# Seven products instead of eight for three retention output units, with sums kept in DRAM, in a one-core hybrid trunk layer

## The chip, the cores and the metric

The kernel runs on one core of one Trainium2 chip. The metric is the device time of one execution in microseconds (us), as the median of several runs. One execution is also recorded by the hardware profiler; all rows of a profile come from that one.

The engines are named as in the profile: PE is TensorE (PEld its weight loads), DVE is VectorE, ACT is ScalarE, POOL is GpSimd, SP is SyncE, whose queue issues nearly all DMA transfers.

## The reference: what is computed

One layer on a sequence of 1024 positions and width 1024, all in float32. Cut to what matters:

```python
h = rms_norm(x, norm1_w)
q, k, v, g_ret, x_lru, y_lru, gate_ret, gate_lru = split(h @ w_in)
o = chunkwise_retention(rotary(q), rotary(k), v)             # 4 heads
y_a = (head_group_norm(o) * silu(g_ret)) @ w_ret_o           # retention output
hl = rg_lru(causal_depthwise_conv(x_lru))                    # recurrent block
y_b = (hl * gelu(y_lru)) @ w_lru_o                           # recurrent output
mix = sigmoid(gate_ret + b0) * y_a + sigmoid(gate_lru + b1) * y_b
x = x + mix @ w_out
h = rms_norm(x, norm2_w)
gate, val = split(h @ ffn_w_up)
x = x + (gelu(conv(gate)) * val) @ ffn_w_down
return rms_norm(x, norm_f_w)
```

The change concerns the product with w_ret_o and the order in which the columns of w_in are worked off.

## The kernel before, in words

**Units and products.** Every large product is cut into units of 256 output channels by all 1024 positions, with 1024 terms to a sum. Activations lie with channels on the partitions, so a unit's operand has four blocks: B11, B12, B21, B22 (first index: half of the terms; second: half of the positions), each of four tiles of 128 x 512. The unit's weights are four blocks A11 to A22 of 128 x 512. Each float32 tile is split into a rounded high part and a rest (`split`: a cast on ACT, a subtraction on DVE), and a product of two tiles is three matmuls (`PASSES`).

A unit runs in one of two forms. `mm_std` computes the four results directly. `mm_fast` uses seven products of blocks in place of eight: the weights give sums S1 to S4, made for each unit on DVE (`preps`, L271 to L287), and the operand gives sums T1 to T4, made once for each operand, when at least one of its units is fast. In the fast form a bank is copied out three times on ACT (`keep`, L432) and three results are summed on DVE (`total`, L443). `FAST_RO` and `FAST_LO` say how many of the four units of the retention output and of the recurrent output are fast: 0 and 3 before.

**Stages.** The input stage has 28 units: eight gate units g, four y and four x units (y_lru and x_lru), and three units for each head h0 to h3. Their order is the string `SEQ`. All are fast but the first two. Then follow the retention output's four units (called o0 to o3 here), the recurrent output's four (l0 to l3), the output projection and the feed-forward part. Between stages the operand changes: the normed input h1 first, then og (the gated retention output, written to the DRAM buffer og_d by `ret_out`), then u (written to u_d by `lru_block`). The results of the gate units go through a sigmoid (`emit_gate`, L1015) to sg_d, those of the y units through a gelu (`emit_y`, L810) to y_d.

**Background work.** The work of the heads and of the recurrent blocks (`rotary_head`, `retention_head`, `ret_out`, `lru_block`) is written as generators, which wait in one line (`back`). After each product of a fast unit, and eight times in a standard unit, `advance(RATE)` lets the first of them go on until its steps have used up a budget of 1 times the number of generators in line. A recurrent block enters the line when its x unit is done; a head's three parts after its three units. `u_start`, which runs after o2, empties the line and then queues the building of u.

A second line, `builders`, makes the operands for the next stage: `operand` reads the 16 tiles of an operand back from DRAM, up to eight tiles ahead, and splits them. It starts for og when the last but one input unit is done (`og_start`). `build` stops while fewer than 20 buffers are free (`RESERVE`); a product that lacks a tile makes it at once (`need`). The instructions of builders, bank copies and totals get a higher priority than their place in the program.

**Buffers and queues.** All tiles of 128 x 512 outside the weights come from one pool of 81 buffers (`U`), used in the order in which they were given back. A full operand with its sums takes 32 + 32 of them. At the last unit on an operand each block is given back after the product that used it; B12 goes before the first fast unit. Each engine works through its instructions in order, and so does SP's queue: a store waiting for its data holds up the loads behind it. Weights (pool `W`) are loaded six tiles ahead.

**Kept sums.** In the feed-forward part the operand of the down projection is a weight. Its sums T1 to T4 are made early by `down_sums`, kept in the DRAM buffer td_d and read back and split by `down_op`. In the profile, x_d and t_d are the buffers x1_d and t1_d of the code.

Of the kernel before, what the change touches and what calls it, by code (L numbers as in the profile page):

```python
# [11 lines left out]
F32 = mybir.dt.float32  # L12
# [5 lines left out]
P = 128  # L18
D = 1024
T = 1024  # L20
KT = 8
TH = 512
# [64 lines left out]
class Units:  # L87
# [11 lines left out]
    def get(self, dt=F32):  # L99
        i = self.q.popleft()  # L100
        self.count += 1
        t = self.pool.tile(self.shape, dt, tag=f"{self.name}{i}", name=f"{self.name}{i}_{self.count}")
        self.at[id(t)] = (i, t)
        return t

    def put(self, *tiles):
        for t in tiles:
            self.q.append(self.at.pop(id(t))[0])
# [28 lines left out]
RESERVE = 20  # L137
LAG, AHEAD_B, AHEAD_T = 2, 7, 4
NOW, SOON, OLD = 3000, 400, 800
FAST_RO = 0  # L140
RO_T = 9
FAST_LO = 3
GQ = False
SEQ = "g g y0 g y1 h0 h1 h2 h3 x0 g g x1 g y2 g x2 g y3 x3"
STD_L = 2


# [1 line left out]
def tile_trunk_layer(ctx, tc, x, xt, positions, params, consts, normf, w_in, w_ro, w_lo,  # L149
                     w_out, w_up, w_dn, w_gate, out):  # L150
    nc = tc.nc
    V, S, G, PE, SY = nc.vector, nc.scalar, nc.gpsimd, nc.tensor, nc.sync
    ST = G if GQ else SY
# [3 lines left out]
    pdr = ctx.enter_context(tc.tile_pool(name="dr", bufs=1, space=bass.MemoryType.DRAM))  # L157
# [6 lines left out]
    get, put = U.get, U.put  # L164
# [3 lines left out]
    ident = cst[:, C_ID:C_ID + P]  # L168

    og_d = pdr.tile([KT, P, T], F32, tag="og", name="og_d")  # L170
    u_d = pdr.tile([KT, P, T], F32, tag="u", name="u_d")
    y_d = pdr.tile([KT, P, T], F32, tag="y", name="y_d")
    sg_d = pdr.tile([2, KT, P, T], F32, tag="sg", name="sg_d")
# [2 lines left out]
    td_d = pdr.tile([3, 4, 4, P, TH], F32, tag="td", name="td_d")  # L176
# [8 lines left out]
    def split(src, get=get, S=S, V=V):  # L185

        hi, lo = get(F32R), get(F32R)
        S.copy(hi, src)  # L188
        V.tensor_sub(lo, src, hi.bitcast(F32))  # L189
        return hi, lo  # L190
# [3 lines left out]
    BS, BV = Behind(tc, S), Behind(tc, V)  # L194
# [112 lines left out]
    builders = deque()  # L307
# [34 lines left out]
    def drain():  # L342
        while back:
            advance(1e9)
# [156 lines left out]
    def pair_src(w, i):  # L501
        return lambda m, kh: w[i, 2 * m + kh]
# [58 lines left out]
    def reads(fetch, keys, ahead):  # L561

        keys, got = deque(keys), deque()
        while keys or got:
            while keys and len(got) <= ahead:
                got.append((state["tick"], fetch(*keys.popleft())))
            yield got.popleft()

    def landed(tick):

        while state["tick"] - tick < LAG and not state["force"]:
            yield 0

    def tsets(op, fetch, ahead=AHEAD_T, here=False):
        tiles = reads(fetch, [(n, j) for j in range(4) for n in ("B11", "B12", "B21", "B22")], ahead)
        for j in range(4):
            four = [next(tiles) for _ in range(4)]
            if not here:
                yield from landed(four[-1][0])
            b11, b12, b21, b22 = (t for _, t in four)  # L580
            t1, t2 = get(), get()
            BV.tensor_sub(t1, b12, b11)
            op["T1", j] = split(t1, get, BS, BV)
            yield 1.2
            BV.tensor_sub(t2, b22, t1)
            op["T2", j] = split(t2, get, BS, BV)
            yield 1.2
            BV.tensor_sub(b12, b12, b22)
            op["T3", j] = split(b12, get, BS, BV)
            BV.tensor_sub(t2, b21, t2)  # L590
            op["T4", j] = split(t2, get, BS, BV)
            put(t1, t2, b11, b12, b21, b22)
            yield 2.4
# [11 lines left out]
    h1, keep = {}, {}  # L605
# [292 lines left out]
    qk, vv, gg = {}, {}, {}  # L898
# [31 lines left out]
    def retention_head(hd, qk, vv):  # L930
        cur = 0
        mask = cst[:, C_MASK + 128 * hd:C_MASK + 128 * hd + 128]
        for h in range(2):
# [55 lines left out]
                yield 0.3  # L989
            put(kd[h], vt[h, 0], vt[h, 1], qk[0, h], qk[1, h])  # L990

    def ret_out(hd, gg):
        for h in range(2):
            for m in range(2):
                ps = psa.get()
                for b in range(4):
                    c0 = 256 * (b % 2) + 128 * m
                    PE.transpose(ps[:, 128 * b:128 * b + 128], ob[h, b // 2][:, c0:c0 + 128], ident)
                g = gg[m, h]
                V.scalar_tensor_tensor(g, ps, pc("ret_gn_w", 2 * hd + m), g, ALU.mult, ALU.mult)  # L1000
                psa.put(ps)
                ST.dma_start(og_d[2 * hd + m, :, TH * h:TH * h + TH], g)
                put(g)
                yield 0.8
            put(ob[h, 0], ob[h, 1])
        if hd == HEADS - 1:
            put(*rot.values())
# [13 lines left out]
    def operand(op, fetch, sums=True):  # L1021

        keys = [(n, j) for n in ("B11", "B21", "B12", "B22") for j in range(4)]
        for key, (tick, t) in zip(keys, reads(fetch, keys, AHEAD_B)):
            yield from landed(tick)
            op[key] = split(t, get, BS, BV)
            put(t)
            yield 0.6
        if sums:
            yield from tsets(op, fetch)  # L1030

    def from_dram(src):
        def fetch(n, j):
            t = get()
            h = int(n[2]) - 1
            SY.dma_start(t, src[4 * (int(n[1]) - 1) + j, :, TH * h:TH * h + TH])
            return t
        return fetch

    og, u = {}, {}  # L1040
# [16 lines left out]
    def emit_ret_o(n):  # L1057
        def emit(m, h, ps, unit):
            ch = 2 * n + m
            t = ojobs[n].take(m, h)  # L1060
            V.tensor_mul(t, ps, t)
            ST.dma_start(t1_d[ch, :, TH * h:TH * h + TH], t)
            put(t)
            if unit is not None:
                put(unit)
        return emit
# [33 lines left out]
    for what in SEQ.split():  # L1100
        if what == "g":
            add_gate()
        elif what[0] == "y":
            n = int(what[1])
# [10 lines left out]
    jobs[-1].last = True  # L1115
    def og_start(post=jobs[-2].post):
        builders.append(operand(og, from_dram(og_d), False))
        return post() if post else None

    jobs[-2].post = og_start  # L1120

    def og_sums():
        drain()
        if FAST_RO:
            builders.append(tsets(og, from_dram(og_d)))

    def u_start():
        drain()
# [1 line left out]

    ojobs = []
    for n in range(4):
        ojobs.append(Job(pair_src(w_ro, n), og, emit_ret_o(n), {2: u_start, RO_T: og_sums}.get(n),
                        fast=n >= 4 - FAST_RO, last=n == 3, drop12=n == 3 - FAST_RO, fetch=from_sg(0, n)))
    for n in range(4):
        ojobs.append(Job(pair_src(w_lo, n), u, emit_lru_o(n), fast=n >= 4 - FAST_LO, last=n == 3,
# [128 lines left out]
    def down_op(g):  # L1265
        def fetch(n, j):
            t = get()
            kh, c = int(n[1]) - 1, int(n[2]) - 1
            SY.dma_start(t, w_dn[8 * g + 4 * kh + j, :, TH * c:TH * c + TH])
            return t  # L1270

        yield from operand(dop[g], fetch, False)

        def sums(n, j):
            t = get()
            SY.dma_start(t, td_d[g, int(n[1]) - 1, j])
            return t

        keys = [(f"T{i}", j) for i in (1, 2, 3, 4) for j in range(4)]
        for key, (tick, t) in zip(keys, reads(sums, keys, AHEAD_B)):  # L1280
            yield from landed(tick)
            dop[g][key] = split(t, get, BS, BV)
            put(t)
            yield 0.6

    def down_sums(g, j):

# [169 lines left out]
```

## Time and profile before

| | us |
|---|---|
| median of 3 runs (1656.72 to 1660.0) | 1659.52 |
| profiled execution, its own time | 1658.44 |
| profiled execution, span from first to last instruction | 1656.7 |

The span is shorter than the execution's own time because it has only what lies between the first and the last instruction. The mean granted clock of PE was 0.997 of full speed.

Where the stages lie in the profiled execution, from PE's timeline:

| stage | from us | to us |
|---|---|---|
| input stage, 28 units | 0 | 657 |
| o0 to o3 and l0 (PE L360, standard form) | 657 | 781 |
| l1 to l3 (PE L417, fast form) | 781 | 844 |
| output projection (PE L1221, its last result added by DVE L1223) | 844 | 938 |

In rows of the profile an instruction carries the line of the kernel that made it, or the line of a helper: L188 and L189 are the two halves of `split`, L122 the same when called for an operand by a builder, L852 the gate matmuls of a recurrent block, L360 and L417 the matmuls of the standard and the fast form. A releaser ("<-ACT u L432") is the instruction that ended the idle time before. Idle time of an engine that is not the bottleneck costs nothing.

### The profile page before, as it was taken

The numbers are of one execution on the slowest core, as the hardware profiler recorded it, in microseconds if no ns is written. First come the engines' busy times: TensorE is split into PE (matmuls) and PEld (weight loads), VectorE is DVE, ScalarE is ACT, GpSimd is POOL, SyncE is SP. The second block draws the span as 40 slices with busy tenths as digits, with TensorE's granted clock in tenths as the row PEclk, the third lists the DMA queues.
The fourth block names the chain that finished last, engine by engine and source line by source line (L and its number), as shares of the span: only waits on it lengthen the run. The fifth ranks groups of instructions, "written<-read, shape, count | busy, mean of one in ns | idle before, by whom it ended". The sixth has DMA issues, their size and how long they took to land. (4 is left out here: it accounts for less than half of the span.)

```text
span 1656.7 us, 21338 instructions
## 1 busy us (share of the span) xinstructions
PE 1622.3 (98%) x7224; PEld 1329.8 (80%) x7224; DVE 1287.0 (78%) x2366; ACT 880.2 (53%) x1480; POOL 40.6 (2%) x60
## 2 busy tenths in 40 slices
PE   8999999999999998999999999999999999999997
PEld 6788888888888877888778778888888887888886
DVE  8998767676888888958871798777777767877786
ACT  7664444535677866853440464444444545453554
POOL 0001000000000000000000000000000000000000
PEclk9999999999999999999999999999999999999999
DMA  8243223131332337658462144444444456778761
GB/s 296 81 161 102 73 68 90 45 96 45 104 119 95 134 122 251 213 171 268 153 215 89 65 150 163 138 134 135 139 143 139 156 160 218 260 262 264 267 203 77
DMA packets 134350, 251.16 MB, mean 152 GB/s; under 512 B 15584, under 2 KB 15712, under 8 KB 134240
## 3 DMA queue, kind: packets, MB, share of 16 engines
q1 hardware_dynamic: 130016, 236.16, 43.9%
q0 software_dynamic: 4224, 13.64, 2.2%
q8 instruction: 56, 0.92, 0.2%
q14 instruction: 54, 0.44, 0.1%
HBM read 177.38 MB, written 67.11 MB: 148 GB/s over the span
## 5 line engine op out<-in xcount | busy, mean ns | idle before, releaser
L417 PE MATMUL g<-u,w 128*128 128x512 f32 x5124 | 1204.0, 393 | 14.9 <-ACT u L432 13.3
L417 PEld LDWEIGHTS g<-u,w 128*128 128x128 f32 x5124 | 958.2, 188 | 218.7 <-ACT u L432 18.6
L188 ACT CAST w<-w 128x512 fp32r<-128x512 f32 x471 | 291.3, 620 | 413.2 <-PE g L417 286.9
L189 DVE TENSOR_TENSOR w<-w,w 128x512 fp32r<-128x512 f32 x471 | 321.9, 684 | 83.4 <-ACT w L188 73.7
L360 PE MATMUL g<-u,w 128*128 128x512 f32 x960 | 223.5, 390 | 0.0
L360 PEld LDWEIGHTS g<-u,w 128*128 128x128 f32 x960 | 179.3, 188 | 38.0 <-ACT u L686 0.3
L443 DVE TENSOR_TENSOR u<-g,u 128x512 f32<-128x512 f32 x183 | 125.3, 685 | 50.5 <-PE g L417 40.4
L432 ACT COPY u<-g 128x512 f32<-128x512 f32 x183 | 106.1, 580 | 65.0 <-PE g L417 62.8
L122 DVE TENSOR_TENSOR u<-u,u 128x512 fp32r<-128x512 f32 (+1 forms) x192 | 122.0, 683 | 15.1 <-ACT u L122 10.4
L122 ACT CAST u<-u 128x512 fp32r<-128x512 f32 x160 | 90.4, 619 | 45.0 <-DVE u L122 15.3
L1221 PE MATMUL g<-u,u 128*128 128x512 f32 x384 | 90.0, 392 | 1.0 <-ACT u L188 0.9
L1221 PEld LDWEIGHTS g<-u,u 128*128 128x128 f32 x384 | 71.3, 188 | 16.6 <-ACT u L188 1.4
L1254 DVE SCALAR_TENSOR_TENSOR u<-u,par,u 128x511 f32<-128x511 f32 x96 | 71.6, 745 | 4.1 <-ACT u L1251 3.4
L1259 POOL DMA_DIRECT2D ff_d<-u x48 | 36.1, 752 | 1251.7 <-DVE u L1258 1251.7
L271 DVE TENSOR_TENSOR w<-w,w 128x512 f32<-128x512 f32 x61 | 42.0, 689 | 25.3 <-DMA w<-ff_d 9.6
L188 ACT CAST u<-u 128x512 fp32r<-128x512 f32 x72 | 43.3, 619 | 26.5 <-DMA u<-w_out 11.2
L1251 ACT ACTIVATE u<-u,par 128x512 f32<-128x512 f32 x48 | 39.2, 817 | 28.2 <-DVE u L443 27.5
L852 PE MATMUL a<-u,u 128*128 128x512 f32 x192 | 48.7, 393 | 2.5 <-ACT u L188 1.6
L189 DVE TENSOR_TENSOR u<-u,u 128x512 fp32r<-128x512 f32 x72 | 47.9, 683 | 4.0 <-ACT u L188 3.7
L1223 DVE TENSOR_TENSOR u<-g,u 128x512 f32<-128x512 f32 x16 | 10.9, 690 | 48.2 <-PE g L1221 48.2
L852 PEld LDWEIGHTS a<-u,u 128*128 128x128 f32 x192 | 35.5, 188 | 12.0 <-ACT u L188 3.1
L274 DVE TENSOR_TENSOR w<-w,w 128x512 f32<-128x512 f32 x61 | 41.9, 687 | 1.0
(175 smaller groups left out, 1211.7 us busy)
## 6 DMA issues: line engine op xcount, KB each, us to landing
w<-w_in SPq DMA_DIRECT2D x112, 256.0 KB, 2.7
w<-w_up SPq DMA_DIRECT2D x96, 256.0 KB, 2.7
u<-w_dn SPq DMA_DIRECT2D x96, 256.0 KB, 3.2
u<-x_d SPq DMA_DIRECT2D x56, 256.0 KB, 5.0
x_d<-u SPq DMA_DIRECT2D x48, 256.0 KB, 3.5
ff_d<-u POOLq DMA_DIRECT2D x48, 256.0 KB, 2.9
td_d<-u SPq DMA_DIRECT2D x48, 256.0 KB, 3.3
w<-ff_d SPq DMA_DIRECT2D x48, 256.0 KB, 4.3
```

Source lines behind the costliest of these rows:

```text
L122: ins = fn(*args, **kw)
L188: S.copy(hi, src)
L189: V.tensor_sub(lo, src, hi.bitcast(F32))
L271: V.tensor_add(s1, a21, a22)
L274: V.tensor_sub(s1, s1, a11)
L360: PE.matmul(ps[h], w[a][:, c], o[b], start=n == 0, stop=n == 23)
L417: PE.matmul(bank, w[a][:, c], need(op, (bn, j))[b], start=first and n == 0, stop=n == 11, skip_group_check=True)
L432: BS.last = S.copy(u, bank).ins.name
L443: BV.last = V.tensor_add(u, bank, u).ins.name
L852: PE.matmul(ps, wg[g][a][:, cs], xs[k][b], start=q == 0, stop=q == 5)
L1221: PE.matmul(ps, o[a][:, 128 * t:128 * t + 128], wo[k][b], start=n == 0, stop=n == 23)
L1254: V.scalar_tensor_tensor(c[:, s:], src[:, :TH - s], w, c[:, s:], ALU.mult, ALU.add)
```

## The change

Three of the four retention output units become fast (`FAST_RO = 3`); o0 stays standard. The sums T1 to T4 of og are not made when og is read back, but in the background line while heads 2 and 3 are finished: `out_sums` reads the tile of head 0 or 1 back from og_d, subtracts it with the two tiles of head 2 or 3, which are still in buffers, and stores four sums to the new DRAM buffer to_d. `kept_sums`, taken out of `down_op` with the same instructions as before, reads them back and splits them after og's own tiles. The order `SEQ` changes: y1 follows y0 at once, x0 to x3 stand three units apart each, and x3 is followed by two gate units that end the stage.

```diff
-FAST_RO = 0
-RO_T = 9
+FAST_RO = 3
...
-SEQ = "g g y0 g y1 h0 h1 h2 h3 x0 g g x1 g y2 g x2 g y3 x3"
+SEQ = "g g y0 y1 h0 h1 h2 h3 x0 y2 g x1 y3 g x2 g g x3 g g"
...
+    to_d = pdr.tile([4, 4, P, TH], F32, tag="to", name="to_d")
...
+    def out_sums(j, b21, b22):
+
+        b11, b12 = get(), get()
+        for h, b in ((0, b11), (1, b12)):
+            SY.dma_start(b, og_d[j, :, TH * h:TH * h + TH])
+        yield 1.0
+        V.tensor_sub(b11, b12, b11)
+        ST.dma_start(to_d[0, j], b11)
+        yield 0.6
+        V.tensor_sub(b12, b12, b22)
+        ST.dma_start(to_d[2, j], b12)
+        put(b12)
+        yield 0.6
+        V.tensor_sub(b11, b22, b11)
+        ST.dma_start(to_d[1, j], b11)
+        put(b22)
+        yield 0.6
+        V.tensor_sub(b21, b21, b11)
+        ST.dma_start(to_d[3, j], b21)
+        put(b21, b11)
+        yield 0.6
+
     def ret_out(hd, gg):
...
                 ST.dma_start(og_d[2 * hd + m, :, TH * h:TH * h + TH], g)
-                put(g)
                 yield 0.8
+                if hd < 2:
+                    put(g)
+                elif h == 1:
+                    yield from out_sums(2 * hd - 4 + m, gg[m, 0], g)
...
+    def kept_sums(op, src):
+
+        def fetch(n, j):
+            t = get()
+            SY.dma_start(t, src[int(n[1]) - 1, j])
+            return t
+
+        keys = [(f"T{i}", j) for i in (1, 2, 3, 4) for j in range(4)]
+        for key, (tick, t) in zip(keys, reads(fetch, keys, AHEAD_B)):
+            yield from landed(tick)
+            op[key] = split(t, get, BS, BV)
+            put(t)
+            yield 0.6
...
         builders.append(operand(og, from_dram(og_d), False))
+        builders.append(kept_sums(og, to_d))
         return post() if post else None
...
-        ojobs.append(Job(pair_src(w_ro, n), og, emit_ret_o(n), {2: u_start, RO_T: og_sums}.get(n),
+        ojobs.append(Job(pair_src(w_ro, n), og, emit_ret_o(n), {2: u_start}.get(n),
                         fast=n >= 4 - FAST_RO, last=n == 3, drop12=n == 3 - FAST_RO, fetch=from_sg(0, n)))
...
+        yield from kept_sums(dop[g], td_d[g])
```

More of the change, by code (lines that the diff above doesn't have):

```diff
@@ L1117, in og_start @@
         builders.append(operand(og, from_dram(og_d), False))
+        builders.append(kept_sums(og, to_d))
         return post() if post else None
     jobs[-2].post = og_start
[L1122 to L1125, printed above, removed]
     def u_start():
@@ L1272, in down_op @@
         yield from operand(dop[g], fetch, False)
[L1274 to L1284, printed above, removed]
+        yield from kept_sums(dop[g], td_d[g])
     def down_sums(g, j):
```

## The prediction

> **What bounds the kernel now.** I read the busy totals first, then the busy time by stretch, then the timeline of TensorE inside the stretches that the diff touches, and last the timelines of ScalarE and SyncE at its longest stop. (The chain of waits is no help here: the pieces it lists start at 1391 us, long after the code that changes.)
>
> ```profile
> span 1656.7 us, 21338 instructions
> ...
> PE 1622.3 (98%) x7224; PEld 1329.8 (80%) x7224; DVE 1287.0 (78%) x2366; ACT 880.2 (53%) x1480; POOL 40.6 (2%) x60
> ```
>
> TensorE (PE) is busy 1622.3 of 1656.7 us; only 34.4 us of the span are not matmuls. VectorE (DVE) is second with 78%. An average can hide a stage with another limit, so here is the run in stretches. The columns are: window, its length, then busy us and (instructions) of PE, weight load, DVE, ACT and POOL, the granted TensorE clock, the DMA share and GB/s.
>
> ```profile
> 20.00:140.00 120.00, 120.00 (x526) 98.18 (x525) 118.57 (x257) 75.31 (x133) 4.29 (x8) 1.00 0.47 156
> 140.00:440.00 300.00, 298.49 (x1424) 246.31 (x1423) 217.90 (x471) 138.55 (x247) 0.00 (x0) 1.00 0.24 70
> 440.00:643.00 203.00, 200.50 (x880) 164.36 (x879) 176.01 (x300) 157.46 (x228) 0.00 (x0) 1.00 0.40 131
> 643.00:657.00 14.00, 9.25 (x34) 7.18 (x33) 8.81 (x15) 8.70 (x17) 0.00 (x0) 0.88 0.87 291
> 657.00:844.00 187.00, 182.51 (x799) 149.08 (x798) 153.41 (x252) 107.51 (x160) 0.00 (x0) 1.00 0.62 202
> ```
>
> They are the start, the four heads, the recurrent blocks, the seam from the input stage to the retention output (o0 to o3), and the two output projections (o0 to o3, then l0 to l3). In every one of them PE is the busiest engine, except at the seam. Two things matter for what follows. DVE at 99% (20 to 140 us) did not cost PE anything: PE was busy 120.00 of 120. And the output stretch already uses 153.41 of 187 us of DVE.
>
> The rows of PE's timeline give the price of a matmul and of the seam (start, length, what, idle time before it):
>
> ```profile
> 571.20 32.80 PE L417 MATMUL g<-u,w 128*128 128x512 f32 x144
> 603.84 0.39 PE L852 MATMUL a<-u,u 128*128 128x512 f32 x1
> ...
> 649.29 4.61 PE L417 MATMUL g<-u,w 128*128 128x512 f32 x12 [4.75 <-ACT u L432]
> ...
> 656.92 6.05 PE L360 MATMUL g<-u,w 128*128 128x512 f32 x26
> ```
>
> From 571.20 to 603.84 run 144 matmuls without a gap: 32.64/144 = 0.2267 us each (the 390 ns of a single record overlap the next one). At the seam PE stands for 4.75 us, and the next twelve take 4.61 us where 12 x 0.2267 = 2.72 are due: 1.9 more. The seam costs 4.75 + 1.9 = 6.6 us. Why it stands, from SyncE and ScalarE:
>
> ```profile
> 635.59 3.95 SPq L1036 DMA_DIRECT2D u<-og_d  x2
> ...
> 642.43 0.50 SPq L811 DMA_DIRECT2D y_d<-u  x1
> ```
> ```profile
> 648.13 0.62 ACT L122 CAST u<-u 128x512 fp32r<-128x512 f32 x1 [3.32 <-DMA y_d<-u]
> 648.66 0.58 ACT L432 COPY u<-g 128x512 f32<-128x512 f32 x1
> ```
>
> The copy that frees PE's bank (L432) stands in ScalarE's queue behind a split of the new operand (L122). That split wants a buffer which a store to y_d still holds, and the store was issued at 642.43, behind reads of og_d. So it is a shortage of buffers at a change of operand, passed on by in-order queues.
>
> **The change, part by part.** *Removed from PE.* A four-bank unit is 2 x 2 x 8 x 3 = 96 matmuls, a seven-product unit 7 x 12 = 84. Three units change: 36 x 0.2267 = **-8.2 us**. This work is on PE, which sets the time in that stretch, so it counts in full unless PE then waits.
>
> *Added to DVE and ACT in the output stage.* Prices:
>
> ```profile
> L188 ACT CAST w<-w 128x512 fp32r<-128x512 f32 x471 | 291.3, 620 | 413.2 <-PE g L417 286.9
> L189 DVE TENSOR_TENSOR w<-w,w 128x512 fp32r<-128x512 f32 x471 | 321.9, 684 | 83.4 <-ACT w L188 73.7
> ...
> L443 DVE TENSOR_TENSOR u<-g,u 128x512 f32<-128x512 f32 x183 | 125.3, 685 | 50.5 <-PE g L417 40.4
> L432 ACT COPY u<-g 128x512 f32<-128x512 f32 x183 | 106.1, 580 | 65.0 <-PE g L417 62.8
> ...
> L271 DVE TENSOR_TENSOR w<-w,w 128x512 f32<-128x512 f32 x61 | 42.0, 689 | 25.3 <-DMA w<-ff_d 9.6
> ```
> ```profile
> 650.59 2.49 DVE L122 TENSOR_TENSOR u<-u,u 128x512 fp32r<-128x512 f32 x4
> ```
>
> Per fast unit: three more splits of weights, four sums of weights (L271 and the like), three bank sums (L443), three bank copies (L432). With 16 splits of the kept sums that is 16 + 3 x 10 = 46 DVE operations. One lasts 0.684 us, but four back to back take 2.49, so the next starts after (2.49 - 0.68)/3 = 0.60: 27.7 to 31.5 us of DVE. ACT gets 25 casts and 9 copies, 25 x 0.62 + 9 x 0.58 = 20.7 us, on top of 107.51 in 187: it does not bind.
>
> *Moved: two gate units behind x3.* Each product spends one unit of budget per waiting background generator, and the steps of one lru_block add up to 35.2. Followed through the old order, o0 starts with 43.0 steps outstanding (7.8 of block 2 and all of block 3); in the new order with 23.8. So 19.2/35.2 = 55% of a block leaves the stretch. The old count is borne out by the blocks' gate matmuls inside it, 66 of the 48 per block, 1.4 blocks against 43.0/35.2 = 1.2:
>
> ```profile
> 657.00:844.00 187.00, 16.21 (x66) 12.31 (x66) 1.00 0.62 202
> ```
>
> What a block costs DVE, from the groups of 440 to 643 us:
>
> ```profile
> L835 DVE SCALAR_TENSOR_TENSOR u<-u,par,u 128x511 f32<-128x511 f32 (+2 forms) x30 | 22.2, 743 | 0.0
> ...
> L864 DVE TENSOR_TENSOR u<-u,u 128x512 f32<-128x512 f32 x10 | 6.9, 689 | 7.7 <-ACT u L855 7.7
> ...
> L885 DVE TENSOR_TENSOR_SCAN u<-u,st,u 128x512 f32<-128x512 f32 x4 | 5.1, 1279 | 0.0
> L872 DVE TENSOR_SCALAR u<-u 128x512 f32<-128x512 f32 x10 | 4.2, 422 | 0.1
> ```
>
> Four tiles, each with three L835, five operations like L864, one L872, one scan and one split: 4 x (2.2 + 3.4 + 0.4 + 1.3 + 0.7) + 2 splits = 33 us, of which 55% are 18. DVE in the stretch becomes 153.4 + 27.7 (31.5) - 18 = 163 to 167 us. PE there becomes 187 - 8.2 - 0.55 x 48 x 0.2267 = 173 us. DVE at 94 to 97% of PE's time: tight, but the row of 20 to 140 us shows PE unhurt at 99%. Without the moved gates DVE would need 181 to 185 against 179 and bind. The PE work of the gates and of the block is only shifted: 0.
>
> *Added in the input stage.* Four out_sums, each two reads of og_d, four subtractions and four stores: 16 subtractions at the price of the like ones for the down weights,
>
> ```profile
> L1299 DVE TENSOR_TENSOR u<-u,u 128x512 f32<-128x512 f32 x12 | 8.3, 689 | 8.6 <-DMA u<-w_dn 8.6
> ```
>
> are 11 us beside 82 us of idle DVE in the heads' stretch (300 - 217.9). SyncE gets 24 issues there and 16 reads of to_d later, at most 0.50 us each by the store above (12 and 8 us), and its stores wait for subtractions with weight loads queued behind them; six weight tiles are loaded ahead, more than a unit's worth (19 us). Hidden: 0, and if that cover fails one stall as at the seam, 6.6. Starting the heads one unit earlier runs them closer to the rotary tables, on a DVE at 99%: 0 by the same row.
>
> *The seams.* (a) Input stage to o0: same mechanism as before, with the sigmoid store of a gate in place of y_d's. Its cost stays; from -6.6 (two gates store and free buffers early) to +6.6 (block 3 is in work at the same time and holds more). I take 0. (b) The kept sums are needed one product after o1 begins. Nearest rows: the same seam at l0 to l1, where sums are made on the spot, and the change of group in the down stage, where they are kept:
>
> ```profile
> 786.71 0.96 PE L417 MATMUL g<-u,w 128*128 128x512 f32 x3 [0.95 <-ACT u L432]
> 788.27 2.60 PE L417 MATMUL g<-u,w 128*128 128x512 f32 x10 [0.59 <-ACT u L122]
> 791.78 44.67 PE L417 MATMUL g<-u,w 128*128 128x512 f32 x194 [0.92 <-DVE u L122]
> 838.47 5.78 PE L417 MATMUL g<-u,w 128*128 128x512 f32 x24 [2.02 <-ACT u L432]
> ```
> ```profile
> 1480.00:1500.00 20.00, 20.00 (x90) 16.22 (x89) 17.68 (x30) 16.81 (x32) 0.00 (x0) 1.00 0.94 308
> ```
>
> 0.95 + 0.59 + 0.92 = 2.5 us against none (1482 us is such a change). DVE is as full as in the first case, the sums kept as in the second: **+1.0**, bounds 0 and 6.6. (c) o3 to l0 is new as a seam: o3 is now fast, its operand is freed only product by product, and u's 32 buffers come from there. Of 81 buffers og takes 24 + 32 after o0, and the block, bank copies and stores take most of the rest, so u can hardly be prefetched any more. Bounds: 0 (the row at 1482) and 6.6 (the seam at 643); nearer to the first, because block 3 ends earlier: **+1.5**.
>
> Does a short stall cost more than itself? After two stops the granted clock fell:
>
> ```profile
> 650.00:654.00 4.00, 4.00 (x13) 3.13 (x13) 3.08 (x6) 2.65 (x6) 0.00 (x0) 0.64 0.75 222
> ```
> ```profile
> 1402.70 7.36 PE L417 MATMUL g<-u,w 128*128 128x512 f32 x24 [1.81 <-ACT u L432]
> ```
> ```profile
> 1404.00:1408.00 4.00, 4.00 (x12) 3.11 (x12) 4.00 (x7) 2.80 (x6) 0.00 (x0) 0.60 1.05 396
> ```
>
> At 1402 a stop of 1.81 us was enough (7.36 us for 24, where 5.44 are due: 1.9 more). The 2.02 at 838 left 24 matmuls at 5.78, nearly on time. So a further 1.9 may come on top of (b) or (c). The Trainium skill (TensorE: Matmul & The Clock Gate, "HAM oscillation") would have only idle gaps over some 3.4 us drop the clock. By it the sum would stand at -5.7 with such stalls; by the row at 1402 it may be -3.8, and the trace contradicts the rule there.
>
> *Sum:* -8.2 + 0 + 1.0 + 1.5 = **-5.7 us**. The span goes from 1656.7 to 1651.0, the profiled execution's 1658.44 to 1652.7. The median of the runs is 1659.52, 1.08 above that execution: **1653.8**.
>
> **Rivals.** *The old seam goes too.* The last two units store early and block 3 no longer follows o0 in full; -6.6 comes on top: -12.3, 1647.2. For it: the stop came from one late store. Against: the store's place behind SyncE's reads is unchanged. *DVE takes over.* If block 3 is not brought forward (its instructions run when DVE has time, not when they are issued), DVE needs up to 185 us against 179: +6.2 and the 2.5 of seams make +0.5, 1660.0, no change. *The buffers run out* (slower): 56 of 81 held through o1 and o2, block 3 still working, each new tile waiting for a store or a product to let go, in-order queues passing that to PE as at 643. It decides if at least two full stops of that kind come new, at o0 to o1 and at o3 to l0: 2 x 6.6 - 8.2 = +5.0, 1664.5. For it: (a) happened with fewer buffers bound. Against: the down stage holds the same sets and shows none at 1482. *The unit count doesn't fall*: excluded, PE's instructions follow the flag.
>
> **How the numbers follow.** Forecast 0.45, its own range 1650 to 1656; seam gone 0.15; DVE takes over 0.13; buffers run out 0.23; 0.04 is left for several stops in the input stage, slower. 0.2% or 3.3 us is about what a measurement here can tell, so faster is under 1656.2, slower over 1662.8. Faster 0.60 and a little from the DVE case: 0.61; same 0.12; slower 0.27. The range of 8 in 10 takes in the seam case in the main and the slow one up to its price: 1645 to 1665.
>
> **What would show it.** Right: PE x7188, L188 and L189 on w x480, L271 x64, L443 x192; about 40 gate matmuls (L852) after o0 starts instead of 66; DVE over 92% busy from o0 to l3 with PE near 98%; stops of 1 to 3 us at o1 and l0. Wrong: an idle PE of over 4 us at o1 or l0 behind ACT L432 or L122 with a DMA as its cause (buffers); PE waiting often and briefly for DVE (DVE bound); losses between 300 and 450 us (stores of the sums holding up weights).

## The result, and the profile after

The changed kernel takes **1679.7 us** (median of 4 runs, 1679.1 to 1681.9) against 1659.4 us for the kernel before on the same chip. The ratio is 1.0122, with a 95% interval of 1.0107 to 1.0137: about 20 us slower, where 1653.8 was forecast. The busy totals of its profiled execution:

```profile
span 1680.2 us, 21455 instructions
...
PE 1625.5 (97%) x7188; PEld 1322.9 (79%) x7188; DVE 1321.3 (79%) x2428; ACT 877.6 (52%) x1499; POOL 40.7 (2%) x60
```

The 36 matmuls are gone (7188), yet PE is busy 3.2 us longer, and outside of matmuls 54.7 us remain (1680.2 - 1625.5), where they were 34.4. So PE stood still for 20 us more, and matmuls that ran took 11 us more than their number accounts for (3.2 + 8.2).

To find the place, the busy time by stretch, first of the kernel before:

```profile
140.00:450.00 310.00, 308.49 (x1468) 254.59 (x1467) 223.48 (x479) 145.75 (x258) 0.00 (x0) 1.00 0.25 74
450.00:640.00 190.00, 187.50 (x823) 153.59 (x822) 167.43 (x286) 148.02 (x213) 0.00 (x0) 1.00 0.39 127
640.00:700.00 60.00, 55.25 (x237) 45.05 (x236) 50.97 (x90) 47.02 (x68) 0.00 (x0) 0.97 0.71 234
700.00:780.00 80.00, 80.00 (x355) 66.24 (x354) 57.05 (x92) 39.92 (x58) 0.00 (x0) 1.00 0.65 214
780.00:870.00 90.00, 84.54 (x365) 67.27 (x364) 75.10 (x121) 41.58 (x75) 0.00 (x0) 1.00 0.59 187
```

The same of the changed kernel:

```profile
140.00:450.00 310.00, 306.21 (x1448) 249.68 (x1447) 232.02 (x496) 147.60 (x259) 0.00 (x0) 1.00 0.30 93
450.00:640.00 190.00, 186.32 (x810) 150.39 (x809) 168.18 (x292) 134.63 (x199) 0.00 (x0) 1.00 0.36 114
640.00:700.00 60.00, 50.34 (x206) 40.04 (x207) 48.92 (x79) 48.08 (x78) 0.00 (x0) 0.91 0.75 246
700.00:780.00 80.00, 73.64 (x302) 58.48 (x301) 66.61 (x113) 44.16 (x73) 0.00 (x0) 0.94 0.68 217
780.00:870.00 90.00, 83.63 (x363) 67.17 (x362) 81.51 (x135) 43.90 (x77) 0.00 (x0) 1.00 0.68 226
```

The number to read is the first one in brackets, the count of matmuls on PE. In equal time the changed kernel gets fewer done. A missing matmul is worth 0.2267 us, the price from the prediction; "lost" below is the length of a stretch less its matmuls at that price (the heads' stretch has small matmuls too, so there only the difference is given, as an estimate).

| stretch, us | lost before | lost after | more |
|---|---|---|---|
| 140 to 450, heads | | | 20 x 0.2267 = 4.5 |
| 450 to 640, recurrent blocks | 3.4 | 6.4 | 3.0 |
| 640 to 700, seam and o0 | 6.3 | 13.3 | 7.0 |
| 700 to 780, o1 to o3 and the change to l0 | -0.5 | 11.5 | 12.0 |
| 780 to 870, most of l0 to l3 | 7.3 | 7.7 | 0.4 |
| the rest, mostly 870 to the end, code unchanged | | | 4.8 |

The last row is what remains: the span grew by 23.5 us, and the 8.2 us of saved matmuls have to be added to it; 31.7 less the rows above is 4.8. (The rows cut both runs at the same clock times, not at the same work.) After 870 us PE's waits behind the bank copies L432 add up to 9.6 us, where they were 5.5. The 11.5 us from 700 to 780 belong to two places, shown below: 4.1 at o1 and 6.6 at the change from o3 to l0.

**The seam.** PE's timeline of the changed kernel at the last input unit:

```profile
663.02 5.48 PE L417 MATMUL g<-u,w 128*128 128x512 f32 x12 [8.86 <-ACT u L432]
```

A stop of 8.86 us where there was one of 4.75, and twelve matmuls at 5.48 us where 2.72 are due. What the copy L432 on ACT stood behind, and what DVE did:

```profile
661.20 0.81 ACT L831 ACTIVATE u<-u,par 128x512 f32<-128x512 f32 x1 [2.90 <-DVE u L885]
662.38 0.59 ACT L432 COPY u<-g 128x512 f32<-128x512 f32 x1 [0.37 <-DVE u L890]
```
```profile
659.89 1.28 DVE L885 TENSOR_TENSOR_SCAN u<-u,st,u 128x512 f32<-128x512 f32 x1
661.08 0.67 DVE L189 TENSOR_TENSOR u<-u,u 128x512 fp32r<-128x512 f32 x1
661.67 0.68 DVE L890 TENSOR_TENSOR u<-u,u 128x512 f32<-128x512 f32 x1
```

The cause is of the predicted kind, with another culprit. In ACT's order the copy comes after the first convolution step of recurrent block 3 (L831), which waits until the last scan of block 2 (L885) is done: by the program L831 writes a new buffer, and the scan is the last to read two that come free. The copy itself then waits for block 2's last product (L890). The most urgent instruction of the kernel hangs on background work that nobody hurries, through the pool of buffers.

**o1.** ACT and PE:

```profile
719.39 0.62 ACT L188 CAST u<-u 128x512 fp32r<-128x512 f32 x1 [1.98 <-DVE u L837]
```
```profile
720.06 1.22 PE L852 MATMUL a<-u,u 128*128 128x512 f32 x2 [2.61 <-ACT u L188]
721.08 3.59 PE L417 MATMUL g<-u,w 128*128 128x512 f32 x11
724.51 1.08 PE L852 MATMUL a<-u,u 128*128 128x512 f32 x4
```

Block 3's second half is at work beside o1 here: its gate matmuls stand in PE's order and wait for a split that waits for the convolution on DVE (L837). The stop is 2.61 us, and the 13 matmuls after it (720.06 to 724.51) take 1.5 us more than the 2.95 that are due: 4.1 us together. DVE has no idle time from 705 us to this stop and beyond:

```profile
705.00:722.00 17.00, 14.39 (x59) 11.25 (x58) 17.00 (x31) 7.04 (x12) 0.00 (x0) 0.93 0.39 127
```

**o3 to l0.** SyncE, ACT and PE:

```profile
761.31 2.21 SPq L1075 DMA_DIRECT2D u<-u_d  x3
763.57 0.42 SPq L1101 DMA_DIRECT2D t_d<-u  x1
```
```profile
767.99 0.62 ACT L122 CAST u<-u 128x512 fp32r<-128x512 f32 x1 [4.49 <-DMA t_d<-u]
```
```profile
768.66 1.22 PE L360 MATMUL g<-u,w 128*128 128x512 f32 x2 [3.75 <-ACT u L122]
769.68 7.84 PE L417 MATMUL g<-u,w 128*128 128x512 f32 x24
777.36 21.55 PE L360 MATMUL g<-u,w 128*128 128x512 f32 x94
```

This is the pattern of the old seam once more: a split of the next operand needs a buffer that a store still holds, and the store was issued behind reads of that operand. The stop is 3.75 us, and the 26 matmuls after it take 8.70 us (768.66 to 777.36) where 5.89 are due: 6.6 us together.

**Heads.** PE near 150 us after the change, and the stretch around it, before (first row) and after:

```profile
147.75 2.11 PE L417 MATMUL g<-u,w 128*128 128x512 f32 x8 [0.67 <-ACT u L432]
150.74 0.66 PE L923 MATMUL a<-cst,u 128*128 128x128 f32 x4 [0.89 <-DVE u L916]
```
```profile
140.00:160.00 20.00, 20.00 (x99) 16.53 (x98) 16.04 (x26) 8.29 (x16) 0.00 (x0) 1.00 0.22 68
140.00:160.00 20.00, 17.54 (x84) 13.25 (x83) 16.58 (x29) 10.25 (x18) 0.00 (x0) 1.00 0.17 53
```

Head 0 comes one unit earlier, and PE waits, among others, for its rotary sums (L916) on DVE.

### The profile page after: what moved, and what is told of

Read it like the earlier page. It is cut to its first block, busy times and chain, and to the rows that moved or that the text cites. A ratio compares the mean times of both kernels' runs of the same rounds, so it can differ in the third digit from the quotient of the medians.

```text
span 1680.2 us, 21455 instructions
## 1 busy us (share of the span) xinstructions
PE 1625.5 (97%) x7188; PEld 1322.9 (79%) x7188; DVE 1321.3 (79%) x2428; ACT 877.6 (52%) x1499; POOL 40.7 (2%) x60
## 4 chain that ended last, share of the span: by engine, by line
issue 52%; PE 37%; DMA 1%; DVE 1%; ACT 1%; POOL 0%; SPq 0%; ACTq 0%; POOLq 0%
PE g L417 34%; PE g L360 3%; DMA w<-ff_d 1%; DVE u L122 0%; DMA ff_d<-u 0%; ACT u L432 0%; ACT a L1390 0%; ACT u L1405 0%; ACT u L122 0%; DVE w L189 0%; ACT w L188 0%; DVE w L271 0%; DVE u L1290 0%; DVE u L1392 0%; DVE u L443 0%
## 5 line engine op out<-in xcount | busy, mean ns | idle before, releaser
L188 ACT CAST w<-w 128x512 fp32r<-128x512 f32 x480 | 296.3, 621 | 422.1 <-PE g L417 325.1
L189 DVE TENSOR_TENSOR w<-w,w 128x512 fp32r<-128x512 f32 x480 | 327.9, 685 | 90.0 <-ACT w L188 85.8
L443 DVE TENSOR_TENSOR u<-g,u 128x512 f32<-128x512 f32 x192 | 131.6, 685 | 50.9 <-PE g L417 41.1
L432 ACT COPY u<-g 128x512 f32<-128x512 f32 x192 | 111.4, 581 | 67.1 <-PE g L417 52.4
L122 DVE TENSOR_TENSOR u<-u,u 128x512 fp32r<-128x512 f32 (+1 forms) x208 | 133.1, 685 | 7.7 <-ACT u L122 4.3
L122 ACT CAST u<-u 128x512 fp32r<-128x512 f32 x176 | 99.4, 619 | 47.9 <-DVE u L122 21.2
L188 ACT CAST u<-u 128x512 fp32r<-128x512 f32 x72 | 43.7, 619 | 39.5 <-DVE u L837 13.2
L271 DVE TENSOR_TENSOR w<-w,w 128x512 f32<-128x512 f32 x64 | 44.1, 689 | 24.4 <-DMA w<-w_up 11.0
L852 PE MATMUL a<-u,u 128*128 128x512 f32 x192 | 52.9, 403 | 7.1 <-ACT u L188 6.6
L189 DVE TENSOR_TENSOR u<-u,u 128x512 fp32r<-128x512 f32 x72 | 47.8, 684 | 2.5 <-ACT u L188 2.3
L1259 DVE TENSOR_TENSOR u<-g,u 128x512 f32<-128x512 f32 x16 | 11.0, 690 | 46.8 <-PE g L1257 46.8
L274 DVE TENSOR_TENSOR w<-w,w 128x512 f32<-128x512 f32 x64 | 43.9, 686 | 0.9
```

Source lines behind the costliest of these rows:

```text
L122: ins = fn(*args, **kw)
L271: V.tensor_add(s1, a21, a22)
L274: V.tensor_sub(s1, s1, a11)
L432: BS.last = S.copy(u, bank).ins.name
L443: BV.last = V.tensor_add(u, bank, u).ins.name
L852: PE.matmul(ps, wg[g][a][:, cs], xs[k][b], start=q == 0, stop=q == 5)
```

## The experiments

Each ratio is to runs of the kernel before in the same session on the same chip.

| run | median, us | ratio to before (95%) |
|---|---|---|
| the change | 1679.7 | 1.0122 (1.0107 to 1.0137) |
| e1, order only | 1667.6 | 1.0045 (1.0031 to 1.0059) |
| e2, fast units and sums, old order | 1688.9 | 1.0175 (1.0143 to 1.0207) |
| e3, sums only | 1664.2 | 1.0030 (1.0015 to 1.0046) |
| e4, two buffers from the weights | 1689.6 | 1.0179 (1.0147 to 1.0210) |
| e5, fewer buffers for the sums | 1671.7 | 1.0089 (1.0066 to 1.0111) |
| e6, less work on DVE | 1673.4 | 1.0087 (1.0070 to 1.0104) |
| e7, both | 1671.9 | 1.0080 (1.0062 to 1.0098) |
| e8, one fast unit | 1669.3 | 1.0067 (1.0052 to 1.0082) |
| e9, sums free of budget | 1671.5 | 1.0075 (1.0046 to 1.0104) |
| e10, own buffers for bank copies | 1684.3 | 1.0154 (1.0127 to 1.0181) |
| e11, e9 and e10 | 1681.2 | 1.0132 (1.0109 to 1.0156) |
| e12, before with own buffers | 1660.5 | 1.0009 (0.9993 to 1.0025) |
| e13, order and sums, no fast unit | 1669.8 | 1.0070 (1.0052 to 1.0088) |
| e14, fast units without operand sums | 1668.4 | 1.0059 (1.0041 to 1.0076) |
| e15, blocks one unit earlier, on e9 | 1673.7 | 1.0093 (1.0075 to 1.0112) |
| e16, a gate back between y0 and y1 | 1679.7 | 1.0134 (1.0096 to 1.0173) |
| e17, the same on e9 | 1678.8 | 1.0125 (1.0097 to 1.0153) |

**What each piece costs: e1, e3, e13, e2.** e1 is the kernel before with the new `SEQ`. e2 is the changed kernel with the old one. e3 and e13 are the changed kernel with the old and the new order and

```diff
-FAST_RO = 3
+FAST_RO = 0
...
-        builders.append(kept_sums(og, to_d))
```

> The kernel before with the new order alone: no unit changes its form and no sums are made. Counted against the matmuls run, the profile of the changed kernel loses 8 us more than before up to the last input unit, 5 at the seam to the retention output, 13 from there to the end of the recurrent output and 5 in code that is the same, and wins 8 by the 36 matmuls. Theory O (the order is at fault: recurrent block 2 or 3 is still at work when the operand changes): the first two losses and part of the third come with the order, 1672 to 1685. Theory B (the fast units are at fault: the sums hold 32 of the 81 buffers while a block runs): 1655 to 1663. If both share it as the ledger says: 1668 to 1674.

> The old order, all four units in the standard form, but the sums of og are still made beside the last two heads and stored (and read by nobody). Both theories: the sums lie beside idle time of VectorE, 1658 to 1662. If their stores hold up the weight loads behind them on SyncE's queue, or the held tiles squeeze the heads: 1664 to 1672, and idle time of TensorE between 300 and 450 us.

> The changed kernel with the old order: three fast units, sums made in the heads and kept, but y3 and x3 end the input stage. Theory B: the losses stay, 1670 to 1682. Theory O: the gain of 8 us of matmuls comes through, 1648 to 1656. Both share it: 1662 to 1670.

> New order and sums made and stored, all four units in the standard form (the sums are read by nobody). If order and sums only add up: 7.9 + 4.5 us, 1670 to 1673, with no stop over 4 us at the last input unit. If the two together make the stop of 8.9 us: 1673 to 1679, and the fast units then cost as much as they save or less.

The order alone costs 0.45% or 7.5 us, which lies between the range in which the order is not at fault and the one in which it has a share; the sums alone cost 0.30% or 5.0 us, at the foot of the range in which they get in the way. PE's idle time from 300 to 450 us is 1.4 us in e3 and 0.4 in the kernel before, so only a small part of the 5.0 is lost there. Together (e13) it is 0.70%, 11.6 us: within the intervals they add up, and before a single unit is fast the kernel has lost more than the fast units can save. The stop at the last input unit is in e13 as well,

```profile
661.73 5.49 PE L417 MATMUL g<-u,w 128*128 128x512 f32 x12 [7.66 <-ACT u L432]
```

and no stop over 3 us near that place in e1 (2.79) or in e3 (2.68): it takes the order and the sums together. The costs add up, as the first of e13's theories has it, but not without the stop. The three fast units then bring the time from 1.0070 to 1.0122, 8.6 us more where 8.2 less were due: 17 us of losses. With the old order they are worse still: e2 lies above every range that was written down, 24 us over e3. The new order does help the fast units, by some 9 us (1.0175 to 1.0122), where the prediction had the moved gates make room for them; it costs 7.5 us where nothing is fast.

**What the fast units lose: e14, e5, e6, e7, e8.** In e14 the sums are never read back:

```diff
-        builders.append(kept_sums(og, to_d))
+        builders.append(no_sums())      # og["T1".."T4", j] = og["B11", j]
```

> The changed kernel, but the sums stored in to_d are never read back or split; the fast units use the tiles of B11 in place of T1 to T4 (values wrong). 32 buffers, 16 splits and 4 MB of reads go, the fast units and their work on the weights stay. If the sums' way back is the whole loss in o1 to o3: the stretch of 700 to 780 us loses under 3 us in place of 11.5, 1665 to 1671. If the fast form itself (three more splits and four sums of weights a unit) is as costly: 1672 to 1679.

The ratio falls from 1.0122 to 1.0059: reading the sums back, splitting and holding them costs 0.63%, **10.4 us**. From 700 to 780 us nothing is lost any more (80 - 351 x 0.2267 = 0.4 us):

```profile
700.00:780.00 80.00, 79.65 (x351) 65.40 (x350) 64.74 (x105) 43.36 (x70) 0.00 (x0) 1.00 0.73 234
```

The stops at o1 and at l0 are both gone. Note DVE: 64.74 us here with PE at 79.65, and 66.61 in the changed kernel with PE at 73.64. Over 80 us DVE is about as busy in both, and in neither case full. The mean hides the 17 us around o1, in which the changed kernel's DVE is full (17.00, above) and e14's is not:

```profile
705.00:722.00 17.00, 16.65 (x74) 13.45 (x73) 11.82 (x19) 13.08 (x18) 0.00 (x0) 1.00 0.79 251
```

Against e13 the fast form as such wins 0.11% or 1.8 us of its 8.2, with overlapping intervals. The traces, one execution of each, show where the rest goes. The output projection begins 8.5 us earlier in e14 than in e13,

```profile
850.03 30.23 PE L1267 MATMUL g<-u,u 128*128 128x512 f32 x125 [2.43 <-ACT u L188]
858.51 5.83 PE L1256 MATMUL g<-u,u 128*128 128x512 f32 x25
```

(e14 first, then e13), and from there to the end it takes 816.9 us (1666.9 - 850.03) against 812.7 (1671.2 - 858.51). So in these two executions the saving arrives, and 4.2 us of it are lost again in code that did not change.

e5 to e7 take the two suspects apart: e5 lets T2 to T4 share T1's buffers, e6 moves 48 subtractions off DVE.

```diff
-            op[key] = split(t, get, BS, BV)
+            pair = split(t, get, BS, BV)                # e5, for T2 to T4
+            put(*pair)
+            op[key] = op["T1", key[1]]
...
+        BS.copy(hi, src)                                # e6, split of og and u
+        BS.copy(lo, src)
```

> The changed kernel, but the four sums of a tile row share the buffers of T1: all 16 sums are read and split as before, the splits of T2 to T4 are given back at once and the products use T1 in their place (values wrong). That leaves 24 more buffers to o1 to o3, about as many as in the kernel before, and VectorE's work unchanged. Theory B (the pool runs out): the stops from o1 to l0 go, some 10 us, 1667 to 1672. Theory D (VectorE's added work is late, and ScalarE's and TensorE's queues stand behind it): no gain, 1677 to 1682.

> The changed kernel, but the second half of each split of og (tiles and sums) and of u's tiles is a second cast on ScalarE in place of a subtraction on VectorE (values wrong). 48 operations leave VectorE, as many as the change adds there; all buffers stay. Theory D: 1660 to 1672. Theory B: 1675 to 1682, or slower, as ScalarE gets 48 casts of 0.62 us.

> Both edits at once. If either cause alone explains the stops, this is no better than the better of the two (within 3 us). If each covers for the other, it is well below both, 1652 to 1662.

> The changed kernel with only o3 in the fast form (24 matmuls more, 5.4 us). The sums are needed when block 3 has ended, but take the same 32 buffers. Theory B: u still can't be fetched ahead and the stop at l0 stays, 1675 to 1682. Theory D: VectorE has 20 operations less and more time for the rest, 1668 to 1675. The two fixed losses that the order and the sums alone showed (7.9 and 4.5 us) set the floor: no better than 1667.

e5 and e6 each win about 0.34% (5.5 us), and from 700 to 780 each halves the loss:

```profile
700.00:780.00 80.00, 75.95 (x326) 61.65 (x325) 69.36 (x116) 52.66 (x81) 0.00 (x0) 0.98 0.81 263
```
```profile
700.00:780.00 80.00, 76.74 (x327) 60.58 (x326) 61.48 (x104) 61.28 (x105) 0.00 (x0) 0.99 0.72 242
```

(the first row is e5, 80 - 326 x 0.2267 = 6.1; the second e6, 80 - 327 x 0.2267 = 5.9.) They halve it in different places. e5, with more buffers, has no stop at the change to l0 any more and 4.05 us at o1; e6, with less work for DVE, has stops of 0.29 and 0.16 us at o1 and still 2.81 at l0:

```profile
720.27 6.48 PE L417 MATMUL g<-u,w 128*128 128x512 f32 x20 [4.05 <-ACT u L434]
```
```profile
777.55 15.10 PE L367 MATMUL g<-u,w 128*128 128x512 f32 x58 [2.81 <-ACT u L122]
```

So the stop at l0 is one of buffers, and the one at o1 one of DVE's order and load. A full DVE by itself is not enough for a stop: in e6 it is busy 16.78 us from 705 to 722, and PE still 16.55. e5 ends within its theory's range; e6 is a little slower than its own allowed, since each theory was to explain the whole loss. Both at once (e7) give no more than either, and the stops that are left are short, behind a bank copy at o1 and a split at l0:

```profile
711.99 3.96 PE L424 MATMUL g<-u,w 128*128 128x512 f32 x16 [1.62 <-ACT u L441]
```
```profile
779.04 3.97 PE L367 MATMUL g<-u,w 128*128 128x512 f32 x16 [1.65 <-ACT u L122]
```

DVE is busy 10.77 us from 705 to 720 there and ACT 12.32. But e6 and e7 give ACT 48 casts that the change does not have, so they can't tell whether this rest belongs to the change or to the edit. e8, with one fast unit, lies where the DVE theory had it and 0.7 us is lost from 700 to 780 (x350): with the sums needed only after block 3 has ended, the collision is gone, and so is, with two fast units fewer, most of the saving.

**The seam: e9, e10, e11, e12.** e9 takes the steps of `out_sums` out of the background line's budget; e10 sets four of the 81 buffers aside for bank copies:

```diff
-        yield 1.0                                       # e9, and each 0.6
+        yield 0.01
...
-NU = 81                                                # e10
+NU = 77
+NK = 4
...
-            u = get()
+            u = K.get() if len(K) and (jb.last or jb in ojobs) else get()
```

> The changed kernel, but a step of out_sums uses 0.01 of the background line's budget instead of 0.6 or 1.0, so that the four sets no longer push the recurrent blocks back by 13.6 steps (over a unit). Theory L (the seam's stop of 8.9 us comes about because block 2 ends later and ScalarE's copy stands behind block 3's first conv, which waits for block 2's last scan): the stop at the last input unit shrinks to that of the order alone (under 3 us), 1670 to 1675. If it's the pool at that place whatever the pace: unchanged, 1677 to 1683; if the sums then crowd VectorE in the heads, more idle time between 300 and 450 us.

> The changed kernel, but four of the 81 buffers are set aside for the bank copies of the last input unit and of the output units (the rest takes them when the pool is empty; the builders' reserve is 16 for 20). Theory P (a bank copy, urgent, is handed a buffer that late background work still holds, and TensorE waits for that work): the stops behind L432 in 640 to 870 us, 14 us, mostly go, 1666 to 1673. Theory Q (the copy only stands behind other instructions in ScalarE's order, which wait for VectorE): the stops stay, 1676 to 1684.

> Both edits. If L and P name different stops: 1660 to 1668. If they name the same: no better than the better of the two.

> The kernel before with four of its 81 buffers set aside for the same bank copies. Theory P: its stop of 4.75 us at the seam goes with its slow matmuls, 1651 to 1655, a version better than before. Theory Q, since there the split and not the copy waits for the buffer: 1657 to 1662.

In e9 the stop of 8.86 us is gone from the last input unit, as theory L had it, and the time with 1.0075 is within its range. But a stop has come up one unit later, in o0:

```profile
672.65 1.22 PE L360 MATMUL g<-u,w 128*128 128x512 f32 x2 [6.08 <-ACT u L122]
```

so the loss from 640 to 700 only falls from 13.3 to 11.0 (x216); the rest of the gain lies from 700 to 780 (5.9 in place of 11.5), where its longest stop is 1.58 us. The gain over the changed kernel is 0.47% or 7.8 us. e10 also shrinks the stop at the last input unit, to 1.32 us behind the copy (now written to the set-aside pool k):

```profile
665.82 5.76 PE L425 MATMUL g<-u,w 128*128 128x512 f32 x24 [1.32 <-ACT k L440]
...
681.59 1.22 PE L860 MATMUL a<-u,u 128*128 128x512 f32 x2 [4.57 <-ACT u L196]
```

Yet the kernel gets no faster (1.0154 against 1.0122, with overlapping intervals): from 450 to 640 us it now loses 11.1 in place of 6.4 (x789), for which the pool, four buffers smaller, would account, and 4.57 us are lost at the next place. Theory P named the stop rightly and its worth wrongly. e11, with both edits, is slower than e9 alone, so the two do not take off different stops. In the kernel before (e12) the same edit removes the old stop of 4.75 us, and the gain is given back elsewhere, in the heads and in the next stage:

```profile
640.00:700.00 60.00, 58.66 (x253) 46.42 (x252) 56.50 (x102) 48.91 (x70) 0.00 (x0) 1.00 0.80 262
700.00:780.00 80.00, 78.31 (x344) 64.15 (x344) 58.40 (x94) 38.54 (x59) 0.00 (x0) 1.00 0.64 215
```

16 matmuls more from 640 to 700, 11 fewer from 700 to 780 (and 8 fewer from 140 to 450); 1.0009 in all, no difference.

**Misses: e4, e15, e16, e17.** e4 moves two buffers from the weights' pool to the common one (83 and 20 for 81 and 22). e15 uses `"... x0 y2 x1 y3 g x2 g g x3 g g g"` on e9, e16 `"g g y0 g y1 h0 ..."` with x3 two units after x2, e17 the same on e9.

> The changed kernel with two buffers more in the common pool (83), taken from the weights' pool (20 for 22). Theory B: the pool is what runs out, so two more make it better by 3 to 10 us, 1670 to 1677, and the stop of 8.9 us at the last input unit shrinks. Theory O, or VectorE as the limit: 1678 to 1684. If the weights needed their two buffers it gets slower than 1684.

> The kernel of e9 with x1, x2 and x3 one unit earlier and three gate units at the end. If what is left there is the collision of block 3 with the sums: 1660 to 1668, and less than 3 us lost from 700 to 780. If the blocks then crowd each other and VectorE before the seam: more lost from 450 to 640, 1672 to 1680.

> The changed kernel with one gate unit back between y0 and y1, as before the change (x3 then stands two units behind x2; two gates still end the stage). If the early heads cost what the heads' stretch shows (4.5 us more lost from 140 to 450, of which 3 with the order alone), that falls by about 3 and TensorE is busy 20 of 20 us around 150 us: 1674 to 1678. If the closer x3 costs as much again at the seam: 1678 to 1684.

> The same on e9 (out_sums takes no budget from the line). If the gains add up: 1666 to 1670. If block 3 comes nearer to the sums by the closer x3: 1671 to 1677.

e4 is slower than the change. The reading written down for that case is that the weights needed their two buffers; its longest stop, 7.06 us, stands before block gate matmuls behind a split, and no run shows how the weights lead to it. e15 shifts the loss rather than ends it: 9.5 us from 700 to 780 (x311), and no better than e9. In e16 the start of the heads is whole again,

```profile
140.00:160.00 20.00, 20.00 (x99) 16.57 (x98) 16.04 (x26) 8.32 (x16) 0.00 (x0) 1.00 0.21 66
```

and the time is no better: 16.1 us are lost from 780 to 870 (x326) in place of 7.7. That x3, now closer, is the reason was expected and is not shown. e17 lies above both of its ranges, with a stop of 8.75 us behind a bank copy at the change from o3 to l0. None of the 17 versions beats the kernel before.

## Why the prediction was wrong

The prediction's sum was -8.2 + 0 + 1.0 + 1.5. Three differences between runs show what its terms came to; they add up to the whole change because each begins where the one before ends. Each is sure to 3 or 4 us, so the middle one is not clear of zero.

| terms | forecast, us | measured, us | from |
|---|---|---|---|
| the early heads, the stored sums, the seam (a) | 0 | +11.6 | e13 against before |
| three fast units | -8.2 | -1.8 | e14 against e13 |
| reading the sums back: (b) and (c) | +2.5 | +10.4 | the change against e14 |
| sum | -5.7 | +20.2 | |

- **The matmuls: right in number.** 7188 on PE; L188 and L189 on weights x480, L271 x64, L443 x192 as counted; 48 gate matmuls of the blocks are left after o0 has begun, where about 40 were expected and 66 had been. In e14's trace the saving arrives at the output projection and is half lost behind it.
- **"Hidden: 0", "0 by the same row" and "(a) ... I take 0": the steps that failed by most.** The sums alone cost 5.0 us (e3), the order alone 7.5 (e1), both 11.6. The sums' subtractions do find room on DVE, as the balance said; what they take up is budget of the background line (13.6 steps): in e9, where they take next to none, 7.8 us come back. The early heads cost 2.5 us of idle PE around 150 us. At the seam the stop went from 4.75 to 8.86 us, and the stretch of 640 to 700 lost 7.0 us more, just over the upper bound of 6.6; block 3's first step in ACT's order, waiting for the end of block 2, is what the rows show. Several stops in the input stage had been left a chance of 0.04; by the rows that stage and its seam lose 14.5 of the 26.9 us lost up to 870.
- **"(b) ... +1.0": another mechanism.** The step looked for a stop when the sums are first needed. The stop at o1 (2.61 us, 4.1 with the slow matmuls, within the bounds) is not a wait for a sum: with the splits of the sums in its order DVE is full for 17 us (11.82 without them, e14), block 3's convolution is late, and PE stands before block 3's gate matmuls. e6, with 48 operations fewer on DVE in all, is nearly free of it.
- **"(c) +1.5": the right mechanism, mis-sized.** The stop is there as described, with 6.6 us, at the upper bound; with 24 buffers more (e5) it is gone. "Nearer to the first, because block 3 ends earlier" did not hold: all 48 gate matmuls of block 3 were still to come when o0 began.
- **"PE unhurt at 99%": the wrong cover.** DVE's work from o0 to l3 came out as counted, 167.1 us (163 to 167 forecast), and yet PE stood still. The row of 20 to 140 us shows that a full DVE can cost PE nothing; it does not show that it must. From 705 to 722 us DVE was full and PE busy 14.39 of 17 us. A balance of busy times can't see which instruction is late, nor waits that run through buffers and in-order queues.
- **The rivals.** The buffers came nearest: of the two places named, o3 to l0 shows the stop described. At o0 to o1 it is DVE, so "DVE takes over" has its part there, over 17 us and not over the whole stretch. Neither rival had a cost in the input stage. As the program hands buffers out, at least 8 of 81 are free during o1, where the kernel before had 29; the same count goes down to 2 in the heads of both kernels with hardly any loss, so the count alone does not make a stop.
- **A reading.** At the seam of the kernel before, too, PE has the most busy time (9.25 of 14 us, DVE 8.81); what sets the seam apart is that no engine is full.
- **Not foreseen:** 4.8 us in code that did not change, by the waits behind L432 named above. That the pool is passed on in another order, with other instructions put beside each other, would account for it; no run shows this.

What stays open is how the 5.0 and 7.5 us split between budget, buffers and DVE, and whether the 16 reads of the sums, which e14 leaves out together with their splits and buffers, have a cost of their own.

## What to carry to other kernels

When one pool serves urgent and background work and is handed out in turn, a copy that frees the bound engine can inherit a buffer from work that nobody hurries; look at what each such copy and split will be handed before adding a resident set, and price every seam at the worst row seen if the pool is nearly empty. Terms that share a cause should be put at the same end of their bounds together. Read the second engine's load around each seam, not only over the stage. And removing one stop is not a gain until the next stretch has been read: in e10 and e12 the stop went and the gain with it, and of the 8.86 us that e9 removed, 6.08 came back one unit later.

## What the runs showed of the hardware

How little idle time can slow the matmuls that follow. In the kernel before a stop of 1.81 us was followed by 24 matmuls that were 1.9 us late. In the changed kernel, by the rows above, it is 13 matmuls 1.5 us late (720.06 to 724.51, where 2.95 are due) after a stop of 2.61 us, and 26 matmuls 2.8 us late after one of 3.75. After 8.86 us the next twelve are 2.8 us late (5.48 for 2.72). The granted clock shows it, here over the 20 us after the stop of 2.61:

```profile
720.00:740.00 20.00, 19.94 (x79) 15.53 (x80) 15.75 (x28) 13.34 (x22) 0.00 (x0) 0.93 0.51 162
```

Such a stop costs 1.5 to 2.8 us on top of itself, and the long one hardly more than the short ones. Not each does: later in the same execution a stop of 2.60 us leaves 24 matmuls at 5.73 us, where 5.44 are due, with the granted clock at 1.00 throughout.

```profile
856.79 5.73 PE L417 MATMUL g<-u,w 128*128 128x512 f32 x24 [2.60 <-ACT u L432]
```

What decides between 2.60 and 2.61 us, no run here shows. The Trainium skill (TensorE: Matmul & The Clock Gate, "HAM oscillation") ties the drop to idle gaps over some 3.4 us; the stops of 1.81 and 2.61 us are under that, and the clock fell. Over the whole execution the mean clock went from 0.997 to 0.991, 0.6% of 1680 or 10 us, which is about the 11 us by which the matmuls took longer than their number says.
